# Layer 0's expert stage: eight experts ranked small in four shared blocks, unsplit products on two column tiles, and the first block's rows picked by products

## The chip, the cores and the metric

One core of a Trainium2 chip runs the kernel. The metric is the device time of one execution in microseconds; the kernel before takes 1118.03 us in the median of three runs.

## The reference

Two layers over 256 latent and 256 context tokens of width 1024. Each layer is a mixer and then a mixture of 16 experts; the routing weights are shared. This case is about the experts of layer 0, which see all 512 tokens:

```python
def moe(h, router_w, router_b, w1, w3, w2):
    scores = jax.nn.sigmoid((h @ router_w).astype(jnp.float32))
    ...                                   # best group of 4, then the top 2 experts in it
    w = w / w.sum(axis=-1, keepdims=True)
    comb = (jax.nn.one_hot(e_idx, N_EXPERTS, dtype=jnp.float32) * w[..., None]).sum(axis=1).astype(h.dtype)
    y = jnp.zeros_like(h)
    for e in range(N_EXPERTS):
        y = y + comb[:, e:e + 1] * ((jax.nn.silu(h @ w1[e]) * (h @ w3[e])) @ w2[e])
    return y
```

Every token goes to two experts, so 1024 places are shared out over 16 experts. Per expert w1 and w3 are 1024 x 512 and w2 is 512 x 1024, all float32: 6 MB, and 96 MB for a layer.

## The kernel before

The kernel keeps its activations transposed in SBUF (XT, 8 x 128 features by 512 tokens). Layer 0's experts are in `moe_rows`. `finish` routes: it leaves for every token and expert a place `pos` (the token's number in that expert's list, or a very large number) and a weight `wts`, and `put_row` writes the normalised rows `halves` to a DRAM buffer `rows` (through buffers called xg).

For each expert e in its own order 0 to 15, one block of 128 slots (CAP) is worked:

- `table(e)` makes four one-hot matrices oh (token to slot, L543) on DVE, multiplies them by `aux` on PE (L551) into the slot's row index and weight, and gathers the rows into XG by an indirect DMA from POOL (L565). It is called four blocks ahead (LEAD).
- `x_turn(e)` transposes the gathered rows on PE (L583) and splits them into xh (rounded to float32r by ACT, L587) and xl (the rest, by DVE, L588).
- `up(e)` multiplies by w1 and w3. Each weight part is split as well, hi on ACT (L286) and lo on DVE (L287), and each product is three: hi·xh, lo·xh and hi·xl (L600 to L602), 48 to an expert.
- `gated(e)` is silu and product, `a_turn(e)` transposes (L612), and `down_(e)` multiplies by w2 in the same three products (L624 to L626), 24 to an expert.
- The first 14 blocks scale the result into ys and add it to a DRAM buffer `yacc` by an accumulating scatter from POOL (L570). The last two (DIRECT) stay on chip and go back to the tokens by products (L756); `yacc` is read back (L736) and added by products with the identity (L762).

The order on PE is up(e), x_turn(e + 1), down_(e - 1) with the silu and transposes of e between. `part()` keeps split weight parts four ahead (LOOK); each of hi and lo has four buffers.

Weights come from SP's queue (L132) in tiles of 1 MB, four for w1 and w3 and two for w2 of an expert, into 12 slots (rings of 6, 5 and 1) that are used in rotation: a load waits until the tile that was in its slot 12 loads earlier has been split. Eleven tiles are issued while the stage before still runs, the twelfth when its buffer comes free.

An expert with more than 128 tokens is finished in a loop on a register (`For_i`, L657), whose count `extra_blocks` works out on DVE; all engines read the count and meet at the loop, whether it turns or not. `table(0)`, its gather and the splits of the first two weight parts (by POOL, PRE) stand ahead of the loop, the first `x_turn` and everything else behind it.

Layer 1's experts (`moe_chip`) already rank the experts that are not fixed by their token count, read their numbers into registers for the loads, and run small experts in 64 columns: two products stand side by side in the two column halves of PE (L859, L898).

Of the kernel before, what the change touches and what calls it, by code (L numbers as in the profile page):

```python
# [16 lines left out]
P = 128  # L17
# [66 lines left out]
def _model(tc, nc, ctx, A, out, dbg):  # L84
# [346 lines left out]
    def extra_blocks(rt, msk, n, cap, tag, more=0):  # L431

        nb, nx = n // P, 2 * n // cap
        cn = pt_([P, NE], tag)
        for b in range(nb):
            PE.matmul(cn, lhsT=ones, rhs=msk[:, b, :], start=(b == 0), stop=(b == nb - 1))
        ext, inc, le = (rt.tile([P, NE], F32, name="ext"), rt.tile([P, NE], F32, name="inc"),
                        rt.tile([P, nx, NE], F32, name="le"))
        V.tensor_scalar(ext, cn, float(cap), None, op0=OP.is_gt)
        for k in range(2, n // cap):  # L440
            V.scalar_tensor_tensor(ext, cn, float(k * cap), ext, op0=OP.is_gt, op1=OP.add)
        V.tensor_tensor_scan(inc, ones[:, 0:NE], ext, 0.0, op0=OP.mult, op1=OP.add)
        V.tensor_tensor(le, inc[:, None, :].to_broadcast([P, nx, NE]), slots[:, 0:nx, None].to_broadcast([P, nx, NE]),
                        op=OP.is_le)
        lst = rt.tile([P, 3, nx], F32, name="lst")
        V.tensor_reduce(lst[:, 0, :], le, axis=AX.X, op=OP.add)
        V.tensor_tensor(le, le, ext[:, None, :].to_broadcast([P, nx, NE]), op=OP.mult)
        V.tensor_reduce(lst[:, 1, :], le, axis=AX.X, op=OP.add)
        V.tensor_tensor(lst[:, 2, :], slots[:, 0:nx], lst[:, 1, :], op=OP.subtract)
        V.tensor_scalar(lst[:, 2, :], lst[:, 2, :], 1.0, float(cap), op0=OP.add, op1=OP.mult)  # L450
        V.tensor_scalar(lst[:, 0, :], lst[:, 0, :], float(NE - 1), None, op0=OP.min)
        ctl = rt.tile([1, nx + 1 + more], I32, name="ctl")
        V.tensor_copy(ctl[:, 0:nx], lst[0:1, 0, :])
        V.tensor_copy(ctl[:, nx:nx + 1], inc[0:1, NE - 1:NE])
        return lst, ctl, nx

    def experts(l):
        down = "e (j p) d -> e p j d" if l == 0 else "e (p j) d -> e p j d"
        return (A["exp_w1"][l].rearrange("e (p j) f -> e p j f", p=P),
                A["exp_w3"][l].rearrange("e (p j) f -> e p j f", p=P),  # L460
                A["exp_w2"][l].rearrange(down, p=P))
# [6 lines left out]
    def expert_tiles(l):  # L468

        w1, w3, w2 = experts(l)  # L470
        for e in range(NE + 1):
            if e < NE:
                for wsrc in (w1, w3):
                    for q in range(2):
                        yield wtile(wsrc[e][:, 4 * q:4 * q + 4, :], 4, F)
            if e:
                for q in range(2):
                    yield wtile(w2[e - 1][:, 2 * q:2 * q + 2, :], 2, D)

    def moe_rows(finish, shift, rows, yacc, fst, st, rt, ahead1, tiles, pull):  # L480
# [18 lines left out]
        pos, wts, msk = finish(rt, put_row, *shift)  # L499
# [3 lines left out]
        if RINGX:  # L503
            ringx = st.enter_context(tc.tile_pool(name="ringx", bufs=RINGX, side="right", reuse_waits="tile"))
            rings[:0] = [ringx] * RINGX
            pull(RINGX)

        aux = rt.tile([P, nb, NE, 4], F32R, name="aux")
        SC.copy(aux[:, :, :, 1], wts)
        GP.memset(aux[:, :, :, 3].bitcast(F32), 0.0)  # L510
        V.tensor_tensor(aux[:, :, :, 2], wts, aux[:, :, :, 1].bitcast(F32), op=OP.subtract)
        V.tensor_tensor(aux[:, :, :, 0], pcol[:, :, None].to_broadcast([P, nb, NE]), pos, op=OP.subtract)
        IDX, WE, XG, XH, XL, H13, AC, AH, AL, BACK, Y = ({} for _ in range(11))

        def parts():

            for e in range(NE + 1):
                if e < NE:
                    for x in range(2):
                        for q in range(4):  # L520
                            if q % 2 == 0:
                                w = next(tiles)
                            yield splitw(w[:, 2 * (q % 2):2 * (q % 2) + 2, :], GP if e == 0 and x == 0 and q < PRE or e and 4 * x + q in PSP else V)
                if e:
                    for q in range(4):
                        if q % 2 == 0:
                            w = next(tiles)
                        yield splitw(w[:, q % 2, :])
# [3 lines left out]
        def part():  # L532

            while len(ahead) <= LOOK:
                nxt = next(source, None)
                if nxt is None:
                    break
                ahead.append(nxt)
            return ahead.pop(0)

        def one_hot(pcol, gp=False):
            oh = wt_([P, P], "oh", F32R)
            (GP if gp else V).tensor_scalar(oh, slots, pcol, None, op0=OP.is_equal)  # L543
            return oh

        def slot_rows(poscol, auxcol, idx, we, gp=False):

            tb = pt_([P, 4], "ad")
            ohs = [one_hot(poscol(b), gp) for b in range(nb)]
            for b in range(nb):  # L550
                PE.matmul(tb, lhsT=ohs[b], rhs=auxcol(b), start=(b == 0), stop=(b == nb - 1))  # L551
            V.tensor_scalar(idx, tb[:, 0:1], home, None, op0=OP.add)
            V.tensor_reduce(we, tb[:, 1:3], axis=AX.X, op=OP.add)  # L553
            return ohs

        def way_back(ohs, back):

            bp = pt_([P, T], "pj")
            for b in range(nb):
                PE.transpose(bp[:, b * P:(b + 1) * P], ohs[b].bitcast(F32), ident)  # L560
            SC.copy(back, bp)

        def gather(idx):
            xg = wt_([P, D], "xg")
# [8 lines left out]
        def table(e):  # L573
            IDX[e], WE[e] = wt_([P, 1], "idx", I32), wt_([P, 1], "we")
            slot_rows(lambda b: pos[:, b, e:e + 1], lambda b: aux[:, b, e, :], IDX[e], WE[e], OHP and e > OHP)
            XG[e] = gather(IDX[e])

        def x_turn(e):
            XH[e], XL[e] = wt_([P, J, P], "xh", F32R), wt_([P, J, P], "xl", F32R)
            for i in range(2):  # L580
                xt = pt_([P, 4, P], "a")
                for j in range(4):
                    PE.transpose(xt[:, j, :], XG[e][:, (4 * i + j) * P:(4 * i + j + 1) * P], ident)  # L583
                s = slice(4 * i, 4 * i + 4)
                if e == i == 0:
                    SC.activation(nothing, xt[:, 0, 0:1], AF.Silu)
                SC.copy(XH[e][:, s], xt)  # L587
                done = V.tensor_tensor(XL[e][:, s], xt, XH[e][:, s].bitcast(F32), op=OP.subtract)  # L588
            return done

        def up(e):
            H13[e] = []
            for _ in range(2):
                h_ = pt_([P, F], "o")
                H13[e].append(h_)
                for kk in range(4):
                    hi, lo = part()
                    for i in range(2):
                        k = 2 * kk + i
                        PE.matmul(h_, lhsT=XH[e][:, k, :], rhs=hi[:, i, :], start=(k == 0), stop=False)  # L600
                        PE.matmul(h_, lhsT=XH[e][:, k, :], rhs=lo[:, i, :], start=False, stop=False)  # L601
                        PE.matmul(h_, lhsT=XL[e][:, k, :], rhs=hi[:, i, :], start=False, stop=(k == J - 1))  # L602

        def gated(e):
            AC[e] = wt_([P, F], "ac")
            SC.activation(AC[e], H13[e][0], AF.Silu)
            V.tensor_tensor(AC[e], AC[e], H13[e][1], op=OP.mult)

        def a_turn(e):
            at = pt_([P, 4, P], "pj")  # L610
            for k in range(4):
                PE.transpose(at[:, k, :], AC[e][:, k * P:(k + 1) * P], ident)  # L612
            AH[e], AL[e] = wt_([P, 4, P], "ah", F32R), wt_([P, 4, P], "al", F32R)
            SC.copy(AH[e], at)
            V.tensor_tensor(AL[e], at, AH[e].bitcast(F32), op=OP.subtract)

        def down_(e):

            yp = [pt_([P, 512], "t") for _ in range(2)]
            for k in range(4):  # L620
                hi, lo = part()
                for c in range(2):
                    s = slice(c * 512, (c + 1) * 512)
                    PE.matmul(yp[c], lhsT=AH[e][:, k, :], rhs=hi[:, s], start=(k == 0), stop=False)  # L624
                    PE.matmul(yp[c], lhsT=AH[e][:, k, :], rhs=lo[:, s], start=False, stop=False)  # L625
                    PE.matmul(yp[c], lhsT=AL[e][:, k, :], rhs=hi[:, s], start=False, stop=(k == 3))  # L626
                yield
            if e < NE - DIRECT:
                ys = wt_([P, D], "ys")
                SC.activation(ys[:, 0:512], yp[0], AF.Copy, scale=WE[e])  # L630
                if YS:
                    SC.activation(ys[:, 512:], yp[1], AF.Copy, scale=WE[e])  # L632
                else:
                    V.tensor_scalar(ys[:, 512:], yp[1], WE[e], None, op0=OP.mult)
                scatter(ys, IDX[e])
            else:
                Y[e] = wt_([P, D], "ys" if e < NE - 1 else "xh", F32R), wt_([P, D], "xg", F32R)
                for c in range(2):
                    yh, yl = (y[:, c * 512:(c + 1) * 512] for y in Y[e])
# [1271 lines left out]
```

## Time and profile before

| | |
|---|---|
| runs, us | 1115.77, 1118.71, 1118.03; median 1118.03 |
| profiled execution, us | 1117.72, with a span of 1115.9 |
| busy in the span, us | PE 1021.4, PE weight loads 696.1, DVE 677.6, ACT 510.5, POOL 111.0 |
| granted TensorE clock over the span | 0.966 of full speed |
| DMA | 310.44 MB, 278 GB/s over the span; weights of experts 190 tiles of 1 MB |
| gathers and scatters in layer 0 | 16 and 14, 15.73 MB |

Rows of instruction groups and of the timeline give the start or the busy time, the mean or duration, engine, line, operation, output and inputs, and shape. A matmul's duration contains its way through the array, so the distance from one start to the next tells its cost. "DMA share" is the mean busy share of the core's 16 DMA engines; a sum of packet times can pass 1. q1 are the plain loads and stores, q0 the gathers and scatters. The chain is the work that ended last, followed backwards, with start and length of each piece.

### The profile page before, as it was taken

The page shows a single profiled execution, that of the slowest core. Times are in us where ns is not written, and L with a number is a line of the kernel's source. Part 1 is how long each engine was busy: PE and PEld are TensorE (multiplying, and loading weights), DVE is VectorE, ACT ScalarE, POOL GpSimd, SP SyncE. Part 2 cuts the span into 40 slices and gives each one's busy share as a digit, 9 for nine tenths or more (in the row PEclk, how much of TensorE's full clock was granted, in tenths as well). Part 3 has the DMA queues.
Part 4 walks back from the last instruction along what each step waited for, and adds up shares of the span by engine and source line. Part 5 has one row for each costly group of instructions (what it writes and reads, how often), then busy time and mean ns, then how long its engine had stood idle before and what let it go on. Part 6 is the DMA issues. An engine that isn't in the chain of part 4 may idle for free.

```text
span 1115.9 us, 15166 instructions
## 1 busy us (share of the span) xinstructions
PE 1021.4 (92%) x5527; PEld 696.1 (62%) x5527; DVE 677.6 (61%) x1471; ACT 510.5 (46%) x857; POOL 111.0 (10%) x93
## 2 busy tenths in 40 slices
PE   4799999999999499999999999799999799988865
PEld 1577845557675378888888887478857444433323
DVE  3543389656777689999999996665666711101111
ACT  2532255337455258888888885433334111111000
POOL 0300000002000322212121110230000100000000
PEclk9799999999999789999999999899999799999988
DMA  9832246582429479999999989580089399999994
GB/s 373 294 125 76 76 172 233 185 305 76 155 82 384 154 268 373 390 392 390 392 384 399 379 326 296 186 303 1 1 312 408 138 420 420 421 420 419 420 421 159
DMA packets 76926, 310.44 MB, mean 278 GB/s; under 512 B 6192, under 2 KB 27952, under 8 KB 50608
## 3 DMA queue, kind: packets, MB, share of 16 engines
q1 hardware_dynamic: 66000, 290.23, 66.0%
q0 software_dynamic: 4320, 15.73, 5.3%
q10 hardware_dynamic: 6528, 3.47, 1.1%
q8 instruction: 45, 0.74, 0.3%
q14 instruction: 33, 0.27, 0.1%
HBM read 295.78 MB, written 13.63 MB: 277 GB/s over the span
## 4 chain that ended last, share of the span: by engine, by line
PE 79%; DMA 8%; DVE 7%; ACT 3%; issue 1%; POOL 0%; ACTq 0%; DVEq 0%; SPq 0%; POOLq 0%
PE pj L1239 13%; PE o L1239 6%; PE o L600 5%; PE o L602 5%; PE o L601 5%; DMA w<-in_exp_w_dram 5%; PE o L859 5%; PE o L235 3%; PE ad L261 3%; PE t L624 3%; PE t L626 3%; PE t L625 3%; PE o L898 2%; PE a L1334 2%; DMA XT<-in_xT_dram 2%; DMA w<-in_ada_w_dram 2%
## 5 line engine op out<-in xcount | busy, mean ns | idle before, releaser
L287 DVE TENSOR_TENSOR lo<-w,hi 128x1024 fp32r<-128x1024 f32 (+2 forms) x266 | 295.9, 1128 | 44.4 <-ACT hi L286 38.3
L286 ACT CAST hi<-w 128x1024 fp32r<-128x1024 f32 (+2 forms) x268 | 259.8, 973 | 123.4 <-PE o L1239 37.8
L600 PE MATMUL o<-hi,xh 128*128 128x512 f32 x256 | 102.0, 398 | 0.1
L602 PE MATMUL o<-hi,xl 128*128 128x512 f32 x256 | 100.9, 394 | 0.5 <-DVE xl L588 0.5
L601 PE MATMUL o<-lo,xh 128*128 128x512 f32 x256 | 101.0, 394 | 0.0
L876 DVE TENSOR_TENSOR ac<-ac,o 64x512 f32<-64x512 f32 x13 | 9.0, 691 | 110.3 <-ACT ac L875 110.3
L859 PE MATMUL o<-w,x 128*64 128x512 f32 x280 | 67.8, 596 | 0.0
L875 ACT ACTIVATE ac<-o 64x512 f32<-64x512 f32 x13 | 7.7, 589 | 107.1 <-PE o L859 63.4
L602 PEld LDWEIGHTS o<-hi,xl 128*128 128x128 f32 x256 | 48.5, 189 | 11.2 <-DVE xl L588 1.1
L600 PEld LDWEIGHTS o<-hi,xh 128*128 128x128 f32 x256 | 48.6, 190 | 10.3 <-ACT xh L587 0.6
L601 PEld LDWEIGHTS o<-lo,xh 128*128 128x128 f32 x256 | 48.5, 190 | 9.8
L261 PE MATMUL ad<-w,sl 128*32 128x512 f32 x320 | 51.3, 626 | 3.6 <-DMA w<-in_ada_w_dram 3.6
L624 PE MATMUL t<-hi,ah 128*128 128x512 f32 x128 | 53.3, 417 | 0.0
L626 PE MATMUL t<-hi,al 128*128 128x512 f32 x128 | 50.6, 396 | 0.0
L625 PE MATMUL t<-lo,ah 128*128 128x512 f32 x128 | 50.5, 395 | 0.0
L1239 PE MATMUL pj<-h_hi,hi 128*128 128x512 f32 x104 | 43.8, 421 | 5.0 <-ACT h_hi L1226 2.6
L859 PEld LDWEIGHTS o<-w,x 128*64 128x64 f32 x280 | 20.6, 137 | 37.9 <-issue 36.3
L1239 PE MATMUL pj<-h_hi,lo 128*128 128x512 f32 x104 | 43.4, 417 | 0.2 <-DVE lo L287 0.2
L1239 PE MATMUL pj<-h_lo,hi 128*128 128x512 f32 x104 | 43.4, 417 | 0.0
L570 POOL DMA_INDIRECT yacc<-ys,idx x14 | 22.1, 1578 | 201.6 <-ACT ys L632 201.6
L235 PE MATMUL o<-w,x 128*32 128x512 f32 x256 | 31.2, 634 | 6.9 <-DMA w<-in_exp_w_dram 6.9
L565 POOL DMA_INDIRECT xg<-rows,idx x16 | 31.5, 1969 | 37.8 <-DVE we L553 17.3
(571 smaller groups left out, 2149.8 us busy)
## 6 DMA issues: line engine op xcount, KB each, us to landing
w<-in_exp_w_dram SPq DMA_DIRECT2D x190, 1024.0 KB, 15.2
w<-in_ada_w_dram SPq DMA_DIRECT2D x48, 1024.0 KB, 6.8
w<-in_even_w_in_dram SPq DMA_DIRECT2D x12, 1024.0 KB, 12.7
w<-in_odd_w_in_dram SPq DMA_DIRECT2D x6, 1024.0 KB, 13.0
XT<-in_xT_dram SPq DMA_DIRECT2D x2, 2048.0 KB, 8.5
w<-in_even_w_out_dram SPq DMA_DIRECT2D x4, 1024.0 KB, 7.5
w<-in_odd_w_out_dram SPq DMA_DIRECT2D x4, 1024.0 KB, 9.3
yacc<-jp ACTq DMA_DIRECT2D x5, 512.0 KB, 9.5
```

Source lines behind the costliest of these rows:

```text
L235: done = PE.matmul(out[32 * q:32 * q + 32, :], lhsT=lhsT, rhs=rhs, start=start, stop=stop)
L261: PE.matmul(ps[32 * q:32 * q + 32, :], lhsT=sl[:, k, :], rhs=w[:, 0, q * 512:(q + 1) * 512], start=(k == 0), stop=(k == J - 1))
L286: SC.copy(hi, w)
L287: eng.tensor_tensor(lo, w, hi.bitcast(F32), op=OP.subtract)
L600: PE.matmul(h_, lhsT=XH[e][:, k, :], rhs=hi[:, i, :], start=(k == 0), stop=False)
L601: PE.matmul(h_, lhsT=XH[e][:, k, :], rhs=lo[:, i, :], start=False, stop=False)
L602: PE.matmul(h_, lhsT=XL[e][:, k, :], rhs=hi[:, i, :], start=False, stop=(k == J - 1))
L624: PE.matmul(yp[c], lhsT=AH[e][:, k, :], rhs=hi[:, s], start=(k == 0), stop=False)
L625: PE.matmul(yp[c], lhsT=AH[e][:, k, :], rhs=lo[:, s], start=False, stop=False)
L626: PE.matmul(yp[c], lhsT=AL[e][:, k, :], rhs=hi[:, s], start=False, stop=(k == 3))
L859: PE.matmul(h[64 * c:64 * c + 64, :], lhsT=x[:, k, :], rhs=ws[c][:, i, :], start=(k == 0), stop=(k == J - 1))
L1239: f = (lambda a, b, **k: PE.matmul(ps, lhsT=b, rhs=a, **k)) if flip else (lambda a, b, **k: PE.matmul(ps, lhsT=a, rhs=b, **k))
```

## The change

Experts 0 and 1 stay fixed, each with a block of 128 slots. The other 14 are ranked by token count on chip (`ranked`, shared with layer 1). The six with the most tokens (lanes 2 to 7) keep blocks of 128 slots and split products. The eight others (lanes 8 to 15) have 64 slots each and go two to a block; their products are plain float32, unsplit, one expert in each column half of PE (`two_halves`). So there are 12 blocks in place of 16. The block order is two large, one shared:

```diff
+    BIG = 6
+    BLOCKS = [(0,), (1,), (8, 9), (2,), (3,), (10, 11), (4,), (5,), (12, 13), (6,), (7,), (14, 15)]
+        def load(self):
+            l, x, q = self.todo.pop(0)
+            w = self.w[x]
+            if l < FIX:
+                src = w[l]
+            else:
+                if l not in self.reg:
+                    c = NX + 1 + l
+                    self.reg[l] = nc.values_load(self.ctl[0:1, c:c + 1], engines=[mybir.EngineType.SP], min_val=0, max_val=NE - 1)
+                src = w[bass.ds(self.reg[l], 1)].rearrange("o p j f -> p (o j) f")
+            m = 4 if x < 2 else 2
+            self.loaded[l, x, q] = wtile(src[:, m * q:m * q + m, :], m, 2048 // m)
...
+        def part():
+            while len(ahead) <= LOOK and None not in ahead:
+                ahead.append(next(source, None))
             return ahead.pop(0)
...
+        def two_halves(out, lhsT, rhs, start, stop):
+            with_last = PE.matmul(out[HALF:], lhsT=lhsT[:, HALF:], rhs=rhs[1], start=start, stop=stop)
+            with tc.issue_after(with_last.ins):
+                PE.matmul(out[0:HALF], lhsT=lhsT[:, 0:HALF], rhs=rhs[0], start=start, stop=stop)
+        def up(i):
...
+                if is_small(i):
+                    if x == 0:
+                        assert part() is None
+                    for q in range(2):
+                        ws = [stream.take(l, x, q) for l in BLOCKS[i]]
+                        for k in range(4):
+                            two_halves(h_, XH[i][:, 4 * q + k, :], [w[:, k, :] for w in ws], q + k == 0, 4 * q + k == J - 1)
+                    continue
```

The register loads take each ranked expert's number from `ctl`. In `parts` a shared block stands as one `None`, over which `part` does not look ahead. A shared block's x and a are not split either. w2 is read with two neighbouring rows to a partition (8 KB in one piece, where it was two of 4 KB), so silu and product write their result with a stride of four (`silu_product`). A shared block's result is scattered in two pieces of 64 rows; the last two blocks, (7,) and (14, 15), stay on chip.

The first block's rows are no longer gathered: `x_first` picks and transposes them from `halves` with 32 products by the one-hots. It stands behind the loop, and the loop's list (`blocks_beyond`, shared with layer 1) now works with a limit for each expert: 128 slots for the fixed two and the six large, 64 for the others. `lpos` and `lwts` are the places and weights in order of rank. One one-hot of 512 columns takes the place of four of 128.

```diff
-        table(0)
-        lst, ctl, nx = extra_blocks(rt, msk, n, CAP, "t")
+        oh0 = table(0)
...
+        rank, perm = ranked(cn, space, ((FIX, 0, DYN),), ctl)
...
+        lst = blocks_beyond(rt, cn, cap, CAP, n, y, ctl)
+        for dst, src in ((lpos, pos), (lwts, wts)):
+            for b in range(0, nb, 2):
+                t = y[:, 0:2 * DYN * DYN].rearrange("p (b r e) -> p b r e", b=2, r=DYN)
+                for i in range(2):
+                    V.tensor_tensor(t[:, i], perm, src[:, b + i, None, FIX:].to_broadcast([P, DYN, DYN]), op=OP.mult)
+                V.tensor_reduce(dst[:, b:b + 2, FIX:], t, axis=AX.X, op=OP.add)
...
         est.close()
+        turned0 = x_first(oh0)
         table(1)
-        turned0 = x_turn(0)
         with tc.issue_after(turned0.ins):
+            put_aux(aux[:, :, FIX:], lpos[:, :, FIX:], lwts[:, :, FIX:])
...
+                    for b in range(nb):
+                        PE.matmul(xt[:, j, :], lhsT=halves[b][:, (4 * h + j) * P:(4 * h + j + 1) * P], rhs=oh[:, b].bitcast(F32),
+                                  start=(b == 0), stop=(b == nb - 1))
```

Three places in the order of instructions matter here (line numbers are each kernel's own). On DVE, what stands between the one-hots of block 0 and the read of the loop's count (TENSOR_LOAD) was, from L442 on:

```order
L442 SCALAR_TENSOR_TENSOR inc<-ones,ext 128x16
L443 TENSOR_TENSOR le<-inc,slots 128x128
L454 CAST ctl<-inc 1x1
L446 TENSOR_REDUCE lst<-le 128x8
L447 TENSOR_TENSOR le<-le,ext 128x128
L451 TENSOR_SCALAR lst<-lst 128x8
L448 TENSOR_REDUCE lst<-le 128x8
L453 CAST ctl<-lst 1x8
L449 TENSOR_TENSOR lst<-slots,lst 128x8
L450 TENSOR_SCALAR lst<-lst 128x8
L654 TENSOR_LOAD ctl
```

and is, after the ranking (ac is its work space) and the list, at its end:

```order
L470 TENSOR_REDUCE lst<-y 128x16
L473 CAST ctl<-lst 1x16
L471 SCALAR_TENSOR_TENSOR lst<-lst 128x16
L793 TENSOR_TENSOR y<-ac,pos 128x196 x2
L794 TENSOR_REDUCE lpos<-y 128x2x14
...
L793 TENSOR_TENSOR y<-ac,wts 128x196 x2
L794 TENSOR_REDUCE lwts<-y 128x2x14
L798 TENSOR_LOAD ctl
```

The places in order of rank, four times two products and a reduction, moved in ahead of DVE's read. On PE, behind the loop, stood the slot table of block 1 and the transposes of block 0:

```order
L657 UNCONDITIONAL_BRANCH
L551 MATMUL ad<-aux,oh 128x4 x4
L583 MATMUL a<-ident,xg 128x128 x8
L600 MATMUL o<-hi,xh 128x512
L601 MATMUL o<-lo,xh 128x512
```

and now stand the 32 products that pick rows, with the slot table of block 1 after them:

```order
L801 UNCONDITIONAL_BRANCH
L672 MATMUL a<-oh,xg 128x128 x32
L609 MATMUL ad<-aux,oh 128x4 x4
L701 MATMUL o<-hi,xh 128x512
L702 MATMUL o<-lo,xh 128x512
```

The products of block 0 moved behind both. On ACT, behind the loop, the changed kernel has two table loads, the weights of the ranked experts for `aux` and two weight splits ahead of the first xh:

```order
L561 ACT_TABLE_LOAD
L561 CAST aux<-lwts 128x4x14
L286 CAST hi<-w 128x1024 x2
L675 ACT_TABLE_LOAD
L675 ACTIVATE nothing<-a 128x1
L651 CAST xh<-a 128x512 x2
L286 CAST hi<-w 128x1024 x4
```

Before, one table load stood there and the xh casts followed it; four casts to hi had been made ahead of the loop, where now two are. On SP the 13 register reads of the later experts stand between the 13th and the 14th weight load of the stage (L509 is the read, L132 the load):

```order
L509 TENSOR_LOAD ctl
L509 ISA x2
L132 ISA
L132 DMA w<-in_exp_w_dram 128x2048
L509 TENSOR_LOAD ctl
L509 ISA x2
```

Before, all loads behind the loop followed each other without reads.

More of the change, by code (lines that the diff above doesn't have):

```diff
@@ L429, in moe_front @@
         return step, finish
[L431 to L441, printed above, removed]
+    FIX = 2
@@ L442, in extra_blocks, with blocks_beyond @@
+    def blocks_beyond(rt, cn, cap, step, n, y, ctl):
+        R = lambda name, *k: rt.tile([P, *k], F32, name=name)
+        over, ext, inc, lst = R("over", NE), R("ext", NE), R("inc", NE), R("lst", 3, NX)
+        V.tensor_tensor(over, cn, cap, op=OP.subtract)
+        V.tensor_scalar(ext, over, 0.0, None, op0=OP.is_gt)
+        for k in range(1, n // step):
+            V.scalar_tensor_tensor(ext, over, float(k * step), ext, op0=OP.is_gt, op1=OP.add)
         V.tensor_tensor_scan(inc, ones[:, 0:NE], ext, 0.0, op0=OP.mult, op1=OP.add)
-        V.tensor_tensor(le, inc[:, None, :].to_broadcast([P, nx, NE]), slots[:, 0:nx, None].to_broadcast([P, nx, NE]),
-                        op=OP.is_le)
@@ L451, in extra_blocks @@
+        V.tensor_reduce(lst[:, 1, :], le, axis=AX.X, op=OP.add)
+        V.scalar_tensor_tensor(lst[:, 2, :], lst[:, 2, :], float(step), lst[:, 1, :], op0=OP.mult, op1=OP.add)
         V.tensor_scalar(lst[:, 0, :], lst[:, 0, :], float(NE - 1), None, op0=OP.min)
[L452 to L455, printed above, removed]
+        V.tensor_copy(ctl[:, 0:NX], lst[0:1, 0, :])
@@ L497, in put_row, with counts @@
                 GP.tensor_tensor(half, half, shift, op=OP.add)
-        pos, wts, msk = finish(rt, put_row, *shift)
+        cn = pt_([P, NE], "pj")
+        def counts(msk):
+            for b in range(nb):
+                PE.matmul(cn, lhsT=ones, rhs=msk[:, b, :], start=(b == 0), stop=(b == nb - 1))
+        pos, wts, msk = finish(rt, put_row, *shift, counts)
         bg(99)
@@ L550, in slot_rows @@
             for b in range(nb):
[L551 to L554, printed above, removed]
+                PE.matmul(tb, lhsT=oh[:, b], rhs=auxcol(b), start=(b == 0), stop=(b == nb - 1))
+            for i in range(m):
+                s = slice(P // m * i, P // m * (i + 1))
+                V.tensor_scalar(idx[s], tb[s, 4 * i:4 * i + 1], home[s], None, op0=OP.add)
+                V.tensor_reduce(we[s], tb[s, 4 * i + 1:4 * i + 3], axis=AX.X, op=OP.add)
@@ L556, in way_back @@
+            return tb
         def way_back(ohs, back):
@@ L571, in scatter, with table @@
                                   in_=ys, in_offset=None, compute_op=OP.add)
[L573 to L580, printed above, removed]
+        def table(i):
+            l, m = BLOCKS[i][0], len(BLOCKS[i])
+            IDX[i], WE[i] = wt_([P, 1], "idx", I32), wt_([P, 1], "we")
+            oh = one_hot(i)
+            tb = slot_rows(oh, lambda b: aux[:, b, l:l + m, :], IDX[i], WE[i], m)
+            if m == 2:
+                IDX2[i] = wt_([HALF, 1], "idx2", I32)
+                V.tensor_tensor(IDX2[i], tb[HALF:, 4:5], home[HALF:], op=OP.add)
+            if i:
+                XG[i] = gather(IDX[i])
+            return oh
@@ L1633, in ahead1 @@
             first_w[c] = wtile(w_in1[:, :, c:c + 256], J, 256, ring)
-    quads = moe_rows(finish, shift_, rows, yacc, fst, st, rt, ahead1, fill(early, tiles0),
-                     lambda n: early.extend(next(tiles0) for _ in range(n)))
+    quads = moe_rows(finish, shift_, rows, yacc, fst, st, rt, ahead1, stream0)
     st.close()
```

377 lines of the change are left out of this document (213 added, 164 removed).

## The prediction

> **What bounds the kernel now.** I read the page's first rows, then busy time by stage, the chain, and the transfers of the stage that the change touches. First, rows of the page and of the chain: the span, and the first and last expert product of layer 0.
>
> ```profile
> span 1115.9 us, 15166 instructions
> ...
> 395.47 0.68 PE o L600
> ...
> 692.06 0.24 PE t L625
> ```
>
> The stage lasts from 395 to 692.5, 297 us of 1115.9; the change touches this stage and the 12 us ahead of it. The profiled execution took 1117.72 us, 1.8 beyond its span and 0.3 under the median of 1118.03; the sum is made against it. Busy time in two stretches (PE, PEld, DVE, ACT, POOL, then granted clock, DMA share, GB/s): layer 0's experts, and layer 1's.
>
> ```profile
> 500.00:550.00 50.00, 50.00 (x241) 41.49 (x239) 48.14 (x62) 42.41 (x50) 10.79 (x6) 1.00 1.03 389
> 900.00:1000.00 100.00, 95.67 (x641) 47.16 (x639) 14.36 (x32) 16.56 (x31) 0.00 (x0) 1.00 1.01 420
> ```
>
> In layer 0 PE never rests, and the DMA share is full as well. Which of them is the bound? Products follow each other at 0.23 us (first three rows), 72 to an expert, with 0.87 us and 0.44 us of transposes:
>
> ```profile
> 668.22 0.39 PE L600 MATMUL o<-hi,xh 128*128 128x512 f32 x1
> 668.45 0.39 PE L601 MATMUL o<-lo,xh 128*128 128x512 f32 x1
> 668.68 0.39 PE L602 MATMUL o<-hi,xl 128*128 128x512 f32 x1
> ...
> 423.25 0.87 PE a L583 x8
> 428.33 0.44 PE pj L612 x4
> ```
>
> That makes 17.9 us; the slot table's four small products bring it to about 18.1. The stage's 297 us hold 16 x 18.1 = 290, so PE is the bound. Now the transfers of 450 to 650, and the queue's wait for slots in 400 to 700:
>
> ```profile
> q1 hardware_dynamic: 11837, 66.99, 81.3%
> q0 software_dynamic: 3024, 11.01, 20.9%
> ...
> w<-in_exp_w_dram SPq DMA_DIRECT2D x66, 1024.0 KB, 14.9
> yacc<-ys,idx POOLq DMA_INDIRECT x11, 10.3
> xg<-rows,idx POOLq DMA_INDIRECT x10, 12.4
> ...
> SPq L132 <- DVE lo L287: 217.6, 82, 5.6
> ```
>
> 66 tiles of 1 MB in 200 us are 11 experts: 18.2 us each, PE's pace; a load waits until DVE has split an old tile. But the engines are never free either. Sharing the 200 us by the two shares (together 102.2%), 66.99 MB or 63.9 tiles take 159.1 us, **2.49 us a tile**, and 21 gathers and scatters take 40.9 us, **1.95 us each**. An expert thus asks 6 x 2.49 + 2 x 1.95 = 18.8 us of transfers against 18.1 us of PE. The backlog shows it: time from issue to landing (min, median, max), of loads issued in 400:415, 625:650 and 650:660:
>
> ```profile
> DMA to landing us min/median/max: 5.9/6.7/8.0
> DMA to landing us min/median/max: 15.2/17.0/18.7
> DMA to landing us min/median/max: 16.4/16.4/16.4
> ```
>
> The transfers fall 10 us behind in 235, and the 12 slots hide it. So the second bound stands 4% behind the first, and what PE saves beyond it cannot be had.
>
> **PE's part.** Eight experts keep split products: 8 x 18.1 = 145 us. Four shared blocks have 24 pairs of unsplit products on two column tiles each. Layer 1 has that form; here are the firsts of two pairs, whose partners on the other column tile start within 0.01 us of them:
>
> ```profile
> 899.47 0.59 PE L859 MATMUL o<-w,x 128*64 128x512 f32 x1
> ...
> 899.89 0.59 PE L859 MATMUL o<-w,x 128*64 128x512 f32 x1
> ```
>
> A pair starts every 0.42 to 0.43 us, so a block is 24 x 0.43 + 1.3 of transposes + 0.3 for its slot table = 11.9 us for two experts, and four are 48. PE falls from 290 to 193 us: 97 us. The 96 splits that go, on ACT and DVE, ran beside PE and count nothing by themselves. The strided silu and product are layer 1's and stand beside the other block's down products: nothing.
>
> **Transfers' part, which becomes the bound.** No weight byte goes. Gathers fall from 16 to 11 (one for each block but the first), scatters from 14 to 10 blocks' worth (three are two of 64 rows). When the engines fill up, in the trace about 430, this has been issued (380:400, 400:415, 415:430):
>
> ```profile
> w<-in_exp_w_dram SPq DMA_DIRECT2D x2, 1024.0 KB, 5.0
> w<-in_exp_w_dram SPq DMA_DIRECT2D x4, 1024.0 KB, 6.7
> w<-in_exp_w_dram SPq DMA_DIRECT2D x6, 1024.0 KB, 7.8
> ...
> 641.94 10.75 SPq L132 DMA_DIRECT2D w<-in_exp_w_dram  x4
> ```
>
> With the 12 loaded ahead that is 24 tiles, of which 3 are still under way at 7.8 us: 75 of 96 remain. Tried on the kernel before: 430 + 75 x 2.49 + 25 x 1.95 = 665.5; the last load, issued at 652.4 and 16.4 us on the way, landed at 668.8, so I add 3. For the changed kernel, blocks 0 and 1 being as before, 17 gathers and scatters remain: 430 + 186.8 + 33.2 + 3 = 653, plus the later start D. Then the last four pairs, 1.7 us: the last product falls at **655 + D**. w2's rows of 8 KB instead of two of 4 KB: layer 1's loads have them, 420 GB/s at share 1.01 or 2.52 us a tile, so nothing.
>
> **The start, D.** Rows of the chain, and of DVE, ACT and the sequencers, around the loop's branch:
>
> ```profile
> 383.48 0.17 DVE L439 TENSOR_SCALAR ext<-t 128x16 f32<-128x16 f32 x1 [1.40 <-PE t L436]
> 386.44 4.88 DMA xg<-rows,idx
> ...
> L657 DVEq EVENT_SEMAPHORE  x11: 21/50/2556, 388.3 to 392.0; - x11
> 390.00:395.00 5.00, 2.37 (x11) 2.37 (x12) 1.16 (x6) 1.63 (x3) 0.82 (x1) 0.50 0.42 113
> 392.08 1.28 ACT L586 ACT_TABLE_LOAD   x1 [10.85 <-DMA xg<-rows,idx]
> 393.64 1.83 PE a L583 x8
> 396.15 0.43 PE o L601
> ...
> L954 SPq TENSOR_LOAD <-ctl x14: 263/267/287, 882.6 to 1064.3; - x14
> L954 SPq SEQ_ASSERT  x14: 18/18/18, 883.5 to 1064.8; - x14
> 881.49 0.35 DVE L1003 TENSOR_TENSOR y<-ac,pos 128x196 f32<-128x196 f32 x1
> 882.50 0.54 DVE L1004 TENSOR_REDUCE pwr<-y 128x28 f32<-128x392 f32 x1
> 886.15 0.42 DVE L1033 TENSOR_TENSOR y<-inc,slots 128x256 f32<-128x256 f32 x1
> ```
>
> All engines meet at the loop. Now DVE is there at 388, the gather lands at 391.3, the loop is left at 392. After the change no gather is under way there; DVE is late instead. From 383.5 it has 13 operations of 196 elements, four reductions of 392, six operations of 256, some twenty small ones and a one-hot of 512 (for which I double the 0.42 less its fixed part): 13 x 0.35 + 4 x 0.54 + 6 x 0.42 + 20 x 0.17 + 0.7 = 13.3, less 1.5 because an operation's end overlaps the next one's start. Done at 395.5; with the step from DVE's last operation to leaving the loop, some 1.5, it is left at 397, 5 later. Then 32 products pick the rows, where 8 transposes stood: at 0.23 each (clock 0.50) 7.4 us, at 0.11 when warm 3.5; I take 6, as they begin cold. ACT queues two table loads, the late experts' weights and two splits (1.28 x 2 + 0.3 + 2.1) ahead of the xh casts; they run beside those products, and are late next if those are quick. First product about 404.5 instead of 395.4. It then runs warm, where now the first ten products take 0.43: 2 us back. But two of the four casts to hi that were made ahead of the loop are now behind it, and DVE has the ranked experts' aux and the one-hots of blocks 2 and 3 between the third and the fifth split part: 1 us lost. **D = 8**, from 3 (warm picks) to 12 (PE waits for the fifth part). SP reads one register ahead of its 13th load and 13 more between it and the 14th; in layer 1 the first read began at 882.6 and its assert came at 883.5, so 0.9 each, 12 us in all, from 398 to 410. The 14th load waits until about 407 for its slot anyway, so 3 us are bare; the backlog of the first blocks takes them up, as PE has 12 tiles in hand. Without that cover they are inside D's range. Three more scatters on POOL cost it 1.6 us each; behind them stand only gathers four blocks ahead.
>
> **Hiccups.** The sum has the engines busy to the last tile. PE has 404 to 655 for its 193 us, 58 to spare; but ACT holds splits of the next big block in its queue ahead of a shared block's silu, PE in turn waits for that silu with its transposes, and old slots come free behind them. At each of the four changes that costs the transfers from 0 (slots enough) to 4 us (the 16.4 us on the way run dry). I take 1 each, 4 in all, nearer to nothing, since layer 1's stage, fed from slots in the same way, keeps its share at 1.01.
>
> **Behind the stage** everything hangs on loads queued after the last expert tile: yacc's two by 5 us later, six of the input projection by 20. They are wanted 4.4 and 19.7 us after the last product, which itself is 2 us after that tile:
>
> ```profile
> 696.87 1.78 PE a L762 x16
> 712.20 2.36 DVE lo L287 x2
> ```
>
> So 0, at most 4 us. Layer 1's ranking is the same operations moved into shared functions: 0.
>
> **Sum.** Last product 655 + 8 + 4 = 667 against 692.5: 25.5 us less; 1117.7 - 25.5 = **1092 us**. Own range: 1080 (D 3, no hiccups, tiles at 2.44) to 1103 (D 12, 10 us of hiccups).
>
> **Rivals.**
> *Lockstep.* A shared block's tiles are freed only as PE passes them, not ahead by splits, and splits stop at a shared block; loads then wait for slots and the engines idle. For it: the 217.6 us of waiting for slots. Against: 12 slots are 30 us of transfers. At 4 us a change, 12 beyond the sum, and D = 12: 1109; with twice as much at a change 1125.
> *The transfers aren't the bound* and PE's 97 us come out: last product at 404 + 193 + 3 = 600, 1026 us. It needs 220 us of transfers in 170; share 1.03 excludes it nearly.
> *The clock* (other side). PE waits inside shared blocks, about 5.0 us for two tiles against 1.7 us of products. At clock 0.50 a product takes 0.43. If it stayed there, 193 us become 360 and the last product falls at 767: 1192 us, slower. It decides where PE's work passes 285 us, mean 0.34 a product. Against it, the starved stage of layer 1 shows:
>
> ```profile
> 1020.00:1030.00 10.00, 7.97 (x61) 2.06 (x53) 1.47 (x4) 0.98 (x3) 0.00 (x0) 0.83 1.01 419
> ```
>
> 0.83 there, 1.00 in most. The Trainium skill (TensorE: Matmul & The Clock Gate, "HAM oscillation — how this bites in real kernels") has idle gaps above 3.4 us halve the clock each time; the 0.50 after the wait at the loop agrees. By that rule alone, an estimate: shared blocks cold, 4 x 10.3 us more, and 3.4 us of each following block at half speed, 7 more: 241 us, still under the 251 that the transfers leave, so this sum stays, and the rival keeps a chance.
> *The loop runs.* Small blocks hold 64 rows. The reference's routing, worked through for its inputs, gives layer 0 the counts 103 and 73 for the fixed two, then 101, 93, 85, 68, 67, 62, and 61 at most for the eight small ones; the loop runs from 65. One turn (a gather of 4.9 us, 6.3 MB at 420 GB/s in series with its products) costs some 35 us: 1127.
>
> **Chances.** Forecast 0.71, lockstep 0.20, no transfer bound 0.02, clock 0.04, loop 0.03. The range 1078 to 1109 takes in the forecast's ends and half of lockstep. Within 0.3% (3.4 us, about what a measurement can tell) falls a bad lockstep: 0.03. Slower 0.06, faster 0.91.
>
> **What would show it.** DMA share about 1.0 from 435 to 660, with some 400 GB/s; expert loads waited for by PE and ACT; SP waiting on PE in shared blocks; the loop left near 397, the first product near 404, the last near 667; 0.43 us a pair. Wrong if the share dips below 0.9 at the shared blocks (lockstep), if PE stays cold in big blocks, or if 2.49 us a tile was set by PE's pace and not by the engines.

## The result, and the profile after

The changed kernel takes 1098.76 us in the median of four runs (1097.89 to 1100.19), against 1118.26 us for the kernel before in the same rounds: a ratio of 0.983, 95% interval 0.981 to 0.985. The forecast was 1092 us, range 1078 to 1109. The profiled execution is the slowest of the four, 1100.19 us with a span of 1098.3; the profiled one of before took 1117.72.

Busy time by stretch, columns as before (the 200 us in the middle of layer 0's experts, the one 20 us in which PE waited longest, and layer 1's experts), then the queues and the issues of the first stretch:

```profile
450.00:650.00 200.00, 188.96 (x882) 117.92 (x880) 109.84 (x128) 97.90 (x121) 25.97 (x18) 0.98 1.02 399
540.00:560.00 20.00, 13.40 (x54) 8.83 (x53) 10.99 (x16) 8.21 (x10) 3.64 (x3) 0.83 1.02 409
900.00:1000.00 100.00, 94.36 (x637) 43.77 (x633) 14.08 (x31) 13.96 (x26) 0.00 (x0) 1.00 1.01 420
...
q1 hardware_dynamic: 9786, 71.23, 85.3%
q0 software_dynamic: 2349, 8.38, 16.4%
...
w<-in_exp_w_dram SPq DMA_DIRECT2D x68, 1024.0 KB, 22.2
yacc<-ys,idx POOLq DMA_INDIRECT x12, 10.2
xg<-rows,idx POOLq DMA_INDIRECT x6, 9.0
```

The DMA share stays at 1.02, also where PE waits: the engines never run dry. Split by shares as in the prediction, 71.23 MB or 67.9 tiles take 200 x 85.3 / 101.7 = 167.8 us, 2.47 us a tile; the 8.38 MB of gathers and scatters, as much as 16 of 128 rows, take 32.2 us, 2.01 each. The prices of before (2.49 and 1.95) held. PE now has idle time, 11 us in 200.

What the weight queue waited for in 400 to 690, and PE and ACT behind the loop:

```profile
SPq L132 <- DMA w<-in_exp_w_dram: 97.0, 46, 3.9
SPq L132 <- DVE lo L287: 60.3, 26, 5.0
SPq L132 <- PE o L683: 27.5, 10, 6.8
...
398.14 9.24 PE L672 MATMUL a<-oh,xg 128*128 128x128 f32 x64 [10.18 <-DVEq L801]
407.14 0.59 PE L609 MATMUL ad<-aux,oh 128*128 128x4 f32 x4
407.58 0.48 PE L701 MATMUL o<-hi,xh 128*128 128x512 f32 x1
...
397.84 1.28 ACT L561 ACT_TABLE_LOAD   x1 [17.33 <-DVEq L801]
407.42 0.59 ACT L651 CAST xh<-a 128x512 fp32r<-128x512 f32 x1 [2.93 <-PE a L672]
```

The largest wait of the queue is no longer for DVE's splits (217.6 us before) but for earlier loads under way. The loop is left at 397.7. The 32 products that pick the rows stand in the trace 64 times and take 9.24 us.

The chain, at the end of the stage and behind it:

```profile
668.62 0.42 PE t L681
669.04 0.66 PE a L909 x2
672.47 1.78 PE a L915 x16
691.47 1.13 PE a L200 x4
695.49 1.85 PE a L261 x2
```

The last expert product begins at 668.6; before it was 692.06. The sums with the identity (L915, L762 before) begin 24.4 us earlier (696.87 before), the statistics (L200) as well (715.86 before), and the modulation's products (L261) only 21.5 (716.98 before).

### The profile page after: what moved, and what is told of

It is laid out like the page before. It is cut to its first block, busy times and chain, and to the rows that moved or that the text cites. A ratio compares the mean times of both kernels' runs of the same rounds, so it can differ in the third digit from the quotient of the medians.

```text
span 1098.3 us, 14558 instructions
## 1 busy us (share of the span) xinstructions
PE 984.2 (90%) x5327; PEld 616.7 (56%) x5327; DVE 559.7 (51%) x1333; ACT 399.6 (36%) x735; POOL 91.1 (8%) x87
## 4 chain that ended last, share of the span: by engine, by line
PE 30%; DMA 14%; DVE 4%; ACT 1%; issue 1%; POOL 0%; SPq 0%; DVEq 0%; ACTq 0%; POOLq 0%
DMA w<-in_exp_w_dram 13%; PE o L1011 5%; PE pj L1358 4%; PE o L235 3%; PE o L1050 2%; PE o L1886 1%; PE t L1358 1%; PE pj L998 1%; PE a L1871 1%; PE a L261 1%; PE o L1358 1%; DVE lo L287 1%; DMA xg<-rows,idx 1%; PE ad L261 1%; PE t L1882 1%; PE t L681 1%
## 5 line engine op out<-in xcount | busy, mean ns | idle before, releaser
L287 DVE TENSOR_TENSOR lo<-w,hi 128x1024 fp32r<-128x1024 f32 (+2 forms) x170 | 179.6, 1077 | 52.2 <-ACT hi L286 45.7
L286 ACT CAST hi<-w 128x1024 fp32r<-128x1024 f32 (+2 forms) x172 | 156.7, 928 | 111.0 <-PE o L1358 37.8
L702 PE MATMUL o<-lo,xh 128*128 128x512 f32 x128 | 51.8, 404 | 6.8 <-DVE lo L287 6.8
L681 PE MATMUL o<-w,xh 128*64 128x512 f32 x128 | 56.2, 595 | 0.1
L683 PE MATMUL o<-w,xh 128*64 128x512 f32 x128 | 56.2, 594 | 0.0
L261 PE MATMUL ad<-w,sl 128*32 128x512 f32 x320 | 50.8, 614 | 3.2 <-DMA w<-in_ada_w_dram 3.1
L701 PE MATMUL o<-hi,xh 128*128 128x512 f32 x128 | 51.6, 403 | 2.2 <-ACT hi L286 1.7
L703 PE MATMUL o<-hi,xl 128*128 128x512 f32 x128 | 50.9, 398 | 0.9 <-DVE xl L652 0.9
L1011 PEld LDWEIGHTS o<-w,x 128*64 128x64 f32 x280 | 20.6, 137 | 37.9 <-issue 36.6
L681 PEld LDWEIGHTS o<-w,xh 128*64 128x64 f32 x128 | 17.0, 137 | 34.6 <-issue 33.4
L1050 PE MATMUL o<-w,at 128*64 128x512 f32 x120 | 33.0, 597 | 0.0
L702 PEld LDWEIGHTS o<-lo,xh 128*128 128x128 f32 x128 | 24.6, 192 | 14.5 <-DVE lo L287 9.7
L701 PEld LDWEIGHTS o<-hi,xh 128*128 128x128 f32 x128 | 24.5, 191 | 9.3 <-ACT hi L286 3.5
```

The lines of the kernel that those rows point to most:

```text
L261: PE.matmul(ps[32 * q:32 * q + 32, :], lhsT=sl[:, k, :], rhs=w[:, 0, q * 512:(q + 1) * 512], start=(k == 0), stop=(k == J - 1))
L286: SC.copy(hi, w)
L287: eng.tensor_tensor(lo, w, hi.bitcast(F32), op=OP.subtract)
L681: with_last = PE.matmul(out[HALF:], lhsT=lhsT[:, HALF:], rhs=rhs[1], start=start, stop=stop)
L683: PE.matmul(out[0:HALF], lhsT=lhsT[:, 0:HALF], rhs=rhs[0], start=start, stop=stop)
L701: PE.matmul(h_, lhsT=XH[i][:, k, :], rhs=hi[:, k % 2, :], start=(k == 0), stop=False)
```

## The experiments

All ratios are to the kernel before, on the same chip. T is the theory that the transfers bound the stage; L the rival that the order of work at the changes between shared and large blocks does.

**Half of the bytes.** Each tile of layer 0's experts loads half of its rows, each used twice.

```diff
-            self.loaded[l, x, q] = wtile(src[:, m * q:m * q + m, :], m, 2048 // m)
+            h = m // 2
+            t = wslot().rearrange("p (a c) -> p a c", a=m)
+            pin(SY.dma_start(t[:, 0:h], src[:, m * q:m * q + h, :]))
...
-                            two_halves(h_, XH[i][:, 4 * q + k, :], [w[:, k, :] for w in ws], q + k == 0, 4 * q + k == J - 1)
+                            two_halves(h_, XH[i][:, 4 * q + k, :], [w[:, k % 2, :] for w in ws], q + k == 0, 4 * q + k == J - 1)
...
```

> The changed kernel, but each weight tile of layer 0's experts brings only half of its rows, and each row is used twice: half of the stage's 96 MB is left out, the work of PE, ACT and DVE stays, and the output is not the reference's. If the transfers bound the stage (T), it falls to PE's pace: some 193 us of products from 407.6, so the last product near 605 and the kernel at 1030 to 1048 us. If the order of work at the changes between shared and large blocks bounds it (L: waits of PE, ACT and the slots on each other), little is gained: 1085 to 1100 us.

Measured: 1076.14 us, ratio 0.963 (0.961 to 0.966), 22.6 less than the changed kernel. Neither number of the expectation came. Its row for 450 to 650, and its first and last expert products:

```profile
450.00:650.00 200.00, 199.92 (x957) 125.68 (x954) 119.13 (x136) 106.67 (x130) 28.47 (x18) 1.00 0.85 262
...
408.15 0.48 PE L704 MATMUL o<-hi,xh 128*128 128x512 f32 x1
...
648.78 0.59 PE L684 MATMUL t<-w,ah 128*64 128x512 f32 x1
```

PE is busy throughout with the engines at 0.85: it is PE-bound, as T says, but PE needs 240.6 us and not 193. The products of one shared block's up part show why (the changed kernel, 440 to 461; columns: count, busy time, mean ns):

```profile
L681 PE MATMUL o<-w,xh 128*64 128x512 f32 x32 | 13.9, 594 | 0.0
L683 PE MATMUL o<-w,xh 128*64 128x512 f32 x32 | 13.9, 594 | 0.0
```

The code issues 16 products to a column half there (two matrices, eight parts of the contraction), the trace has 32: every plain float32 product runs as two passes of 0.43 us. A block is 48 pairs of passes, not 24: 20.6 us, not 10.3.

**Twice the pairs.** Each pair of a shared block is issued twice.

```diff
-            with_last = PE.matmul(out[HALF:], lhsT=lhsT[:, HALF:], rhs=rhs[1], start=start, stop=stop)
...
+            for r in range(2):
+                s0, s1 = start and r == 0, stop and r == 1
+                with_last = PE.matmul(out[HALF:], lhsT=lhsT[:, HALF:], rhs=rhs[1], start=s0, stop=s1)
...
```

> The changed kernel, with each pair of products of layer 0's shared blocks issued twice (the output is not the reference's). That adds 4 x 24 x 0.43 = 41 us to PE and nothing to the transfers. If the transfers bound the stage (T), all of it is hidden but what stands behind the last expert tile, at most one block's 24 pairs: 1099 to 1109 us. If PE's order bounds it (L), it comes out in full: about 1140 us.

Measured: 1159.35 us, ratio 1.037 (1.035 to 1.040), 60.6 more. Neither number of the expectation came here either. With two passes the edit adds 4 x 48 x 0.43 = 82.6 us to PE, not 41. So 22 us of them were hidden, and the rest came out:

```profile
450.00:650.00 200.00, 200.00 (x958) 113.75 (x956) 94.71 (x111) 84.31 (x102) 23.14 (x15) 1.00 0.93 344
```

PE is busy throughout again, and from its first to its last expert product the kernel takes 323.1 us, which is the 240.6 with half of the bytes and the 82.6 added. The two experiments bracket the same distance from both sides: PE alone would be done 22 us before the transfers let it (22.6 taken away with the bytes, 82.6 - 60.6 hidden). Some 20 of the 22 lie between the first and the last expert product, where the changed kernel takes 260.9 us, the rest behind the stage.

**Half of the pairs.** Every second product of a shared block is left out, all tiles are loaded.

```diff
-                        for k in range(4):
+                        for k in (0, 2):
...
-                            two_halves(yp[c], AH[i][:, k, :], [w[:, s] for w in ws], k == 0, k == 3)
+                        if k % 2 == 0:
+                            two_halves(yp[c], AH[i][:, k, :], [w[:, s] for w in ws], k == 0, k == 2)
```

> The changed kernel, with every second pair of products of layer 0's shared blocks left out (the output is not the reference's); all bytes are still loaded. The trace shows each of these products as two passes of 0.43 us, so PE loses 4 x 24 x 0.43 = 41 us. If the transfers alone bound the stage (T), only what stands behind the last tile gets shorter (7 us to some 2 to 3): 1092 to 1097 us. If PE's pace, 246 us with the pairs, shares in setting the end (P), more comes out: 1088 us or less. If nothing changes, 1099, the tail is not PE's work.

Measured: 1095.23 us, ratio 0.981 (0.978 to 0.983): some 3 less than the changed kernel (3.5 in the medians, 2.3 to 2.9 by the ratios), T's number. The last four expert loads on SP, of this kernel and of the changed one, and PE in one stretch of this kernel:

```profile
632.30 8.87 SPq L132 DMA_DIRECT2D w<-in_exp_w_dram  x4
...
632.68 8.68 SPq L132 DMA_DIRECT2D w<-in_exp_w_dram  x4
...
500.00:540.00 40.00, 23.29 (x89) 15.17 (x90) 15.37 (x19) 14.75 (x18) 3.85 (x3) 0.81 1.02 396
```

With 41 us of PE's work gone, the last tile is asked for at the same time (641.2 and 641.4), and PE idles 17 of 40 us while the engines stay full. This is the transfers' bound itself; what was gained lies behind the last tile (landed at 663.5, last product over at 666.2).

**The kernel before with half of the bytes**, the same edit as the first.

> The kernel before, with half of the rows in each weight tile of layer 0's experts, each used twice (half of the bytes left out, the output is not the reference's). If the products bound the stage before (T: 16 x 18.1 = 290 us of PE), nothing is gained: 1113 to 1120 us. If the transfers already bounded it there, which would make 2.49 us a tile a price set by the engines and not by PE's pace, it falls by 10 us or more.

Measured: 1118.35 us, ratio 1.000 (0.998 to 1.002). PE bounded the stage before, and the bytes were free there.

**The start.** Four kernels move it. In the first, block 0 is gathered ahead of the loop again; in the second, the places in order of rank stand behind the loop; the third does both. The changed kernel ran beside them.

```diff
-            if i:
-                XG[i] = gather(IDX[i])
+            XG[i] = gather(IDX[i])
...
-        turned0 = x_first(oh0)
         table(1)
+        turned0 = x_turn(0)
```

```diff
-        for dst, src in ((lpos, pos), (lwts, wts)):
...
         est.close()
+        for dst, src in ((lpos, pos), (lwts, wts)):
...
```

> The changed kernel once more, unaltered, as the base for the three others on the same chip: 1097 to 1100 us.

> The changed kernel, with the first block's rows gathered by the indirect DMA ahead of the loop and transposed behind it, as before, in place of the 32 products that pick them. If the picks' 9.2 us are the mis-sized term and a later start moves the end one for one (T), the 8 transposes of 1.8 us and the xh casts let the first product start at about 404 instead of 407.6: about 1095 us. If the pick saves the gather's latency at the loop, undoing it costs up to 5 us: 1104. If 12 loaded tiles hide the start (H), nothing changes: within 1 us of the changed kernel.

> The changed kernel, with the places and weights in order of rank (8 products of 196 elements and 4 reductions on DVE, about 5 us) moved from ahead of the loop to behind it. If a later start moves the end one for one (T), the loop is left about 5 us sooner, at 392.7, and the kernel takes about 1094 us. If 12 loaded tiles hide the start (H), it takes the same within 1 us. If DVE's work behind the loop is what PE then waits for, less than 2 us are gained.

> Both edits together: first block gathered and transposed, and the places in order of rank behind the loop. If the two waits stand one behind the other (T), the gains add: the loop left at 392.7, the first product at about 398 to 400, the kernel at 1090 to 1092 us. If ACT's queue behind the loop (a table load of 1.28 us, the late weights, two splits of 1.05 us) is next, the first product is at 401 or later and the gain at most 6 us: 1093 or more.

The fourth, which came last, takes the list out of the way too; the loop makes it for itself if it turns.

```diff
-        lst = blocks_beyond(rt, cn, cap, CAP, n, y, ctl)
+        lst, rest = blocks_beyond(rt, cn, cap, CAP, n, None, ctl, True)
...
         with tc.For_i(0, todo, 1) as it:
+            rest(wt_([P, T], "y"))
```

> The kernel that gathers the first block and ranks late (1092.7 us), with all of the loop's list but its count (11 operations on DVE, 3.4 us from 388.65 to 392.1) moved into the loop, which does not turn here. The loop should be left near 390 instead of 393.5. If the start still moves the end one for one, the first product comes at about 395.4 instead of 398.7 and the kernel takes 1089 to 1090.5 us. If the gather, which lands at about 391, or ACT's queue (two table loads and two splits, 4.7 us, ahead of xh) is what is late next, 1 us or less comes out: 1091.5 to 1093.

Measured, with times from each one's trace (the start of the product, the issue of the load):

| kernel | loop left | first product | 20th weight load | last product | median us | ratio (95%) |
|---|---|---|---|---|---|---|
| changed | 398.2 | 408.0 | 431.9 | 668.7 | 1098.94 | 0.983 (0.981 to 0.985) |
| gathered first | 398.1 | 403.6 | 429.6 | 668.7 | 1096.22 | 0.979 (0.977 to 0.981) |
| ranks late | 392.7 | 403.0 | 426.8 | 664.6 | 1095.97 | 0.980 (0.977 to 0.982) |
| both | 393.4 | 398.8 | 426.2 | 663.1 | 1092.70 | 0.977 (0.975 to 0.979) |
| both, list late | 391.1 | 396.5 | 423.1 | 661.8 | 1089.90 | 0.975 (0.973 to 0.977) |

The start is not hidden behind the 12 loaded tiles. But the end goes rather with the 20th load, where the queue runs at the engines' pace, than with the first product: gathering gives 4.4 us at the first product and 2.3 at the 20th load. The clock takes the difference. PE and the granted clock in 405 to 410, the changed kernel first, then gathered first:

```profile
405.00:410.00 5.00, 5.00 (x39) 4.66 (x38) 2.46 (x7) 0.87 (x2) 1.20 (x1) 1.00 0.01 2
405.00:410.00 5.00, 5.00 (x15) 3.91 (x14) 3.73 (x7) 1.91 (x2) 0.00 (x0) 0.59 0.27 58
```

The picks, slow as they are, leave PE at full clock. In the profiled execution of gathered first even these 2.3 us were gone at the last product. The lead was down to 1.0 at 605, after a stretch at clock 0.50 around 550 that lasted 10.2 us instead of 6.8; the rest went behind two short waits (0.86 and 0.76 us) at 614 to 617 that both kernels have; the changed kernel first, then gathered first:

```profile
618.00:620.00 2.00, 1.69 (x8) 1.08 (x7) 1.97 (x3) 2.00 (x3) 0.82 (x1) 1.00 1.00 418
618.00:620.00 2.00, 2.00 (x6) 1.28 (x6) 2.00 (x3) 1.59 (x2) 0.00 (x0) 0.50 1.01 422
```

So its 2.7 us in the median are not shown to come from the start. For the three others the medians (3.0, 6.2 and 9.0 us less than the changed kernel) go with the 20th load (5.1, 5.7 and 8.8 sooner) and the last product (4.1, 5.6 and 6.9), so T's order holds, though not one for one; the first two lie 0.7 to 2 us above T's numbers. The times also hold something that is not the start's. From the issue of layer 1's last expert load to the end of the last instruction the five profiled executions take 32.9, 28.9, 32.8, 30.5 and 28.9 us, in the order of the table. So gathered first, 3.6 us shorter in its span with the same last product, has all of that from layer 1's end, and the last kernel 4.0 of 10.8. In the last kernel the loop is left when the gather lands:

```profile
391.21 1.28 ACT L286 ACT_TABLE_LOAD   x1 [10.82 <-DMA xg<-rows,idx]
```

That transfer is late next, as its second theory has it; of the 3.4 us 2.3 came at the loop and 2.8 in the median, which is the first theory's number. By the ratios it is 2.1, and the two intervals overlap. It is the fastest kernel of this case: 28 us below the one before, 9 below the changed one.

**Two that build on "both".** One keeps PE busy at the loop with seven unused products, six of them with the identity, to have it warm; the other puts the ranks behind the first block's xl on DVE.

```diff
+        warm = pt_([P, T], "o")
+        first = PE.matmul(warm[0:NE], lhsT=inc, rhs=XT[:, 0, :], start=True, stop=True)
+        with tc.issue_after(first.ins):
+            for _ in range(6):
+                PE.matmul(warm, lhsT=ident, rhs=XT[:, 0, :], start=True, stop=True)
         todo = nc.values_load(ctl[0:1, nx:nx + 1], min_val=0, max_val=nx)
```

```diff
         with tc.issue_after(turned0.ins):
+            for dst, src in ((lpos, pos), (lwts, wts)):
...
             put_aux(aux[:, :, FIX:], lpos[:, :, FIX:], lwts[:, :, FIX:])
```

> The kernel that gathers the first block and ranks late (1092.7 us), with seven plain float32 products of the identity, unused, on PE while it waits at the loop. If the missing gain of its earlier start is the clock (C: its first products ran at 0.50 to 0.59 where the 32 picks had brought PE to 1.00), the first ten products come at 0.23 us instead of 0.43 and 2 to 3 us more come out: 1090 us. If DVE's xl, which stands behind the ranks, is what PE waits for there (D), or the start no longer matters, the same within 1 us: 1092 to 1093.5.

> The kernel that gathers the first block and ranks late (1092.7 us), with the places in order of rank behind the first block's xl on DVE instead of ahead of it. There PE waited 1.2 us for xl at 400.0, and the first split parts queue behind. If DVE's queue is what PE waits for at the start (D), 1.5 to 3 us come out: about 1090.5 us. If the clock is (C), or the start no longer matters, the same within 1 us: 1092 to 1093.5.

Measured: 1098.47 us, ratio 0.982 (0.981 to 0.984), 5.8 slower than "both"; and 1093.27 us, 0.979 (0.977 to 0.981), not told apart from "both". The first failed by its own making. PE's extra products, and what ACT waited for:

```profile
389.76 6.20 PE L800 MATMUL o<-XT,ident 128*128 128x512 f32 x12
...
393.49 1.28 ACT L286 ACT_TABLE_LOAD   x1 [12.78 <-DVEq L799]
396.74 1.28 ACT L286 ACT_TABLE_LOAD   x1 [16.71 <-PEq L804]
...
398.00:400.00 2.00, 2.00 (x11) 2.00 (x12) 1.40 (x6) 1.99 (x3) 0.78 (x1) 0.55 0.55 115
```

They ran until 396.0, two passes each, and everyone waited for PE at the loop (the ACT rows are "both", then this one: 3.2 us later). By the time the first block's rows were there, the clock was down again, to 0.55 in 398 to 400. Whether a warm start is worth 2 us is therefore not answered. The second has its first product at 398.6 and its 20th load at 426.1, as "both" (398.8 and 426.2). PE's wait of 1.2 us for xl at 400 is gone, but PE waits 1.0 us for DVE's lo at 411.0 and 1.6, where it was 0.7, for the next xl at 417.5. So moving the ranks in DVE's queue gained nothing; that the queue as a whole sets the start is neither shown nor ruled out.

**The tail.** The last but one block's down products, loads and all, go ahead of the last block's up products.

```diff
+                both = (up(i) if i < len(BLOCKS) else []), (down(i - 1) if i > FIX else [])
+                self.todo += both[1] + both[0] if i == len(BLOCKS) - 1 else both[0] + both[1]
...
+            if i == n_ - 1:
+                for _ in dn:
+                    pass
+                up(i)
```

> The changed kernel, with the down products of the last but one block (loads and all) ahead of the up products of the last shared block, so that fewer products stand behind the last tile: eight passes of 0.43 us, 3.4, in place of 7. If the last tile (landing at 661.7) and the work behind it set the end (T), the last product comes at about 665, 3 to 4 us sooner: about 1095 us. If the loads behind the stage set what follows (B), at most 1 us: 1098 or 1099. If the silu of the last block now stands bare on PE (S), nothing is gained or up to 2 us lost: 1099 to 1101.

Measured: 1101.72 us, ratio 0.985 (0.983 to 0.987): nearest to S, 0.7 beyond its range. The interval overlaps the changed kernel's, so a loss is not shown. In its profiled execution the loop was left 2.1 us later already, and from first to last product it took 260.6 us, the changed kernel 260.7. Nothing was gained. S's reason is only a small part of it: PE waits 0.9 us for the last silu's product, at 662.2. In the changed kernel's trace PE waits 1.7 us in all between 620 and 669 (0.9 at 636, 0.5 at 653, 0.3 at 659), so its products nearly follow each other, whatever their order. That the two bounds run side by side near the end is a reading of this, not tested by itself.

## Why the prediction was right, and where not

- **The bound passes from PE to the transfers: shown.** Bytes were free before and cost 22 us after; PE work was taken away without moving the last load. The prices of a tile and of a gather held (2.47 and 2.01 us).
- **PE's 193 us: wrong.** "A pair starts every 0.42 to 0.43 us, so a block is 24 x 0.43": the rows of layer 1 quoted for that are passes, two to a product, and 48 pairs of passes make a block. That is 41 us of the error. It is 240.6 us from first to last product, with 20 us to spare where the sum had 58. The total survived since the transfers still end later: the margin was large enough, not the term right. The Trainium skill (Perfetto Trace Analysis, "Engine Utilization") halves the array's rate for float32 in a low and a high part. A pass of 0.43 us, where a float32r product takes 0.23, agrees; that a product takes two such passes is what the trace shows beyond it.
- **The start: the loop right, the picks too small.** Left at 397.7 (397 forecast). The picks took 9.24 us, not 6, beyond the upper bound of 7.4, again for two passes a product. First product 407.6, not 404.5. Against the kernel before that is 12.2 us later, the 14th load 12.4 and the 20th 11.0, where D was 8 with a range to 12. SP's register reads (to 406.5) were hidden, as forecast: the 14th load then waited 4.7 us more for its slot.
- **Hiccups: 4 forecast, 0 measured.** The DMA share lies between 1.00 and 1.04 in every 10 us from 440 to 670. The last two loads were issued at 640.2 and 641.0 and took 19.9 and 21.6 us, so the last landed at 662.6, not at 665 (the 661.7 in an expectation goes by the middle of the two):

```profile
DMA to landing us min/median/max: 19.9/20.8/21.6
```

- **The tail: 2 us forecast, 6.4 measured.** One block's down products are 16 pairs of passes, and they stand behind the block before and its put-back. This term more than took back what the earlier last tile gave: last product over at 669.0, forecast 667. That the two nearly cancel is luck.
- **Behind the stage: 0 forecast, 4.2 measured**, just past its bound of 4. The lead of 24.4 us shrinks to 21.5 at the modulation's products and to 20.2 at layer 1's attention. From the sums to the first of the modulation's products it is 20.2 us before, 23.1 after, and 20.2 and 20.4 in the kernels with half of the bytes and with twice the pairs, where the engines are not full. In the changed kernel the first three tiles of the modulation's weight land from 3.3 us ahead of the statistics to 2.5 behind them, before from 11.9 to 0.7 ahead. So these loads come late, and the stage's backlog, which lies ahead of them, fits as the reason.
- **Layer 1's end: 0 forecast, 2.6 in the profiled execution** (the lead of 20.2 us is 17.6 at the end of the span). From the issue of the last expert load to the end of the last instruction it is 33.0 us in the changed kernel, 29.5 before, and 28.9 to 33.2 in the experiments. The last 32 us, before and after:

```profile
1084.00:1116.00 32.00, 19.39 (x129) 9.85 (x125) 6.58 (x15) 2.60 (x5) 0.00 (x0) 0.89 0.50 191
1066.00:1098.00 32.00, 19.45 (x112) 9.72 (x102) 5.70 (x13) 2.60 (x5) 0.00 (x0) 0.85 0.43 160
```

  The clock is lower where the end is longer, here 0.85 against 0.89; what decides it was not tried and stays open.
- **The sum**, against the profiled 1100.19: the stage's end 2.0, less 0.9 since fewer put-back products stand between it and the sums; behind it 4.2, at the end 2.6: 7.9 of 8.2. The median lies 6.8 above the forecast.
- **The rivals.** Lockstep did not come: the engines never idle. The clock fell to 0.50 once between 402 and 688, from 548.8 to 555.6, around PE's one long wait (5.7 us; 540 to 560, 0.83). The loop did not turn.

## What to carry to other kernels

Before a duration is multiplied by a count of products, count the rows of one such group in the trace against the code: a float32 product may be two. When two bounds stand within a few per cent, taking away half of each in turn tells both in two runs, and a gain promised by one ends where the other begins; here 97 us of promised PE time were 49, and 23 came out at the stage's last product. What then paid here was the time at which the binding resource first runs full, which what stood in line ahead of the stage had set. Before a small gain in the total is put down to an edit, see in the trace where it arises: here up to 4 us came and went at layer 1's end, which no edit touched.

## What the runs showed of the hardware that was not expected

- A transpose of 128 x 128 appears once in the trace, a plain float32 product of that size twice: 8 transposes took 1.97 us at clock 0.50, 32 products 9.24 us at 0.50 and then 1.00.
- Waits of 0.86 and 0.76 us at 614 to 617 were followed by a clock of 0.50 for 3.4 us in one kernel (gathered first) and of 1.00 in another (the changed one) with the same waits. The Trainium skill (TensorE: Matmul & The Clock Gate, "HAM oscillation — how this bites in real kernels") puts the limit at idle gaps of about 3.4 us; here shorter ones sometimes sufficed, and the measurement decides.
